# A hybrid encoder layer: all 16 gate jobs of the second batch as 2x2 block products, with their first two products made at the end of the convolutions

## The chip, the cores and the metric

The kernel runs on one core of one Trainium2 chip. The time is device microseconds of one execution. Five engines work in queues of their own: TensorE (PE in the profile, with its weight loads as PEld), VectorE (DVE), ScalarE (ACT), GpSimd (POOL) and SyncE (SP), which here only issues transfers. Each engine takes its instructions in the order in which they stand in its queue.

## What is computed

One encoder layer runs over two batches (prompt and sample, 1024 positions of 1024 channels each). What matters of the reference:

```python
xn = rmsnorm(x, g_pre)
p = xn @ w_in
fv, fg, hv, hg, mg = jnp.split(p, ...)          # Fourier, its gate, Hyena, its gate, merge gates
fz = fft over sequence and channel of fv, real part
y_f = (fz * silu(fg)) @ w_fourier_out
v, x1, x2 = jnp.split(short_conv(hv, w_short), 3, axis=-1)
z = v
for n, gate in enumerate((x1, x2)):
    z = gate * long_conv(z, kf[:, n], hyena_d[n])
y_h = (z * silu(hg)) @ w_hyena_out
g_f, g_h = jnp.split(sigmoid(mg + b_merge), 2, axis=-1)
out = (g_f * y_f + g_h * y_h) @ w_out
y = x + rmsnorm(out, g_post)
```

The change is about the gate columns of `xn @ w_in` for the second batch: the sections 0 (`fg`), 4 (`hg`), 5 and 6 (`mg`), each 1024 channels wide.

## The kernel before

Every float32 product is made of three matmuls on rounded halves (high x high, high x low, low x high). A matrix operand is therefore first split: ACT casts it to the high part (`wh`, `bh`, `yh`), and DVE or POOL subtracts to get the low part (`wl`, `bl`, `yl`). `split` does both.

Three phases follow each other. `phase_fourier` makes the Fourier branch. `phase_main` makes filters and the first batch's gates, and then, in `branches`, the long convolutions of both batches: 16 steps (two orders, eight channel tiles) for each batch. A step is a projection (`inproj`, PSUM tile `pin`), transposes (`tph`), forward transforms (`pX`), a product with the filter on DVE (`t`, `y`), backward transforms (`pT`) and sums on DVE (`S`, `T1s`, `U`, `q`, `ez`, `yc`) up to the gated `x`. `phase_tail` makes the second batch's gates, then four net products (`pn`), then the output rows.

A gate can be made in two ways. `spill_gate` makes one tile (128 channels, 1024 positions) from 48 matmuls with `inproj`, in a `pin` tile: two quarters of four blocks of w_in, each split once for 24 matmuls. A gate job of `phase_tail` makes two tiles (`c`, `c + 1`) as a 2x2 block product with seven products instead of eight, 12 matmuls each: 84. The seven are 11 x B11, 12 x B21, s2 x T2, s1 x T1, s4 x B22, s3 x T3, 22 x T4. The left ones are blocks of w_in and their sums, made by `prepare` from a raw tile `wraw`; B11, B21 and B22 are quarters of the normed input `X` (tiles x0k for the first half of the positions, x1k for the second); T1 to T4 are sums of them, loaded into four `room` tiles. `times` makes one product.

Eight single tiles of the sections 5 and 6, the list `PLAIN`, are made by `spill_gate` in the last four convolution steps and behind them; the other 24 tiles are 12 gate jobs. The block sums of w_out for the last product (`block_sums`, tiles `ws`) are called inside the gate loop.

Most of the program is written in the order of the work, and a scheduler with a model of its own then places the instructions of each engine; it may draw an instruction ahead of others written before it. `issue_after` and `keep_in_program_order` bind it: `times` holds its first matmul in program order, while the `mm3` matmuls of `inproj` are free. Tiles are taken from pools by tag, with a fixed number of buffers (`bufs`); a new tile waits for the last reader of the old one under its tag.

Of the kernel before, what the change touches and what calls it, by code (L numbers as in the profile page):

```python
# [9 lines left out]
F32 = mybir.dt.float32  # L10
# [151 lines left out]
class K:  # L162
# [35 lines left out]
    def setup(self, ctx):  # L198
        tc, nc, a = self.tc, self.nc, self.a
        self.cp = cp = ctx.enter_context(tc.tile_pool(name="cp", bufs=1))  # L200
        self.ps = ctx.enter_context(tc.tile_pool(name="ps", bufs=2, space=bass.MemoryType.PSUM))
        self.dr = ctx.enter_context(tc.tile_pool(name="dr", bufs=1, space=bass.MemoryType.DRAM))

        def ld(name, shape, src, eng=nc.sync):
            t = cp.tile(shape, F32, name=name)
            eng.dma_start(t, src)
            return t
        self.ident = ld("ident", [P, P], a["c_id"], nc.gpsimd)
        self.gpre = ld("gpre", [P, 8], a["g_pre"], nc.gpsimd)
# [20 lines left out]
        self.d_s = [[dt(f"d_s{n}_{p}", [P, 4, 512]) for p in range(7)] for n in range(2)]  # L230
        self.d_wo = [dt(f"d_wo{k}", [P, D]) for k in range(8)]
        self.d_sh = [[dt(f"d_sh{b}_{k}", [P, L]) for k in range(8)] for b in range(NB)]

# [822 lines left out]
            nc.sync.dma_start(self.d_g[b][sec][ct][:, s], t)  # L1056


    def conv_front(self, u, ws):
        nc = self.nc  # L1060
        u4 = u.rearrange("p (n s) -> p n s", n=4)
        eo = ws.tile([P, 2, 4, P], F32, tag="t4", name="eo4", bufs=2)
        self.add("dve", eo[:, 0], u4[:, :, P:2 * P], u4[:, :, P - 1::-1])
        self.sub("dve", eo[:, 1], u4[:, :, P:2 * P], u4[:, :, P - 1::-1])
        xt = ws.tile([P, 2, 4, P], F32, tag="t4", name="xt", bufs=2)
        for e in range(2):
            tp = self.psum("T", 2, "tph")
            for q in range(4):
                nc.tensor.transpose(tp[:, q * P:(q + 1) * P], eo[:, e, q], self.ident)  # L1069
            nc.scalar.copy(xt[:, e].rearrange("p a b -> p (a b)"), tp)  # L1070
        return self.butterfly(ws, xt, xt)
# [133 lines left out]
    def branches(self, nb, nct, ws, mi):  # L1205
# [5 lines left out]
        for b in range(nb):  # L1211
# [4 lines left out]
        plain = list(self.PLAIN)  # L1216
        Z, X, G = {}, {}, {}

        def front(i):
# [34 lines left out]
        for i, (b, n, c) in enumerate(steps):  # L1254
# [20 lines left out]
            if b == 0 and NF <= c:  # L1275
                self.spill_gate(0, 0, c, ws)
        with tc.issue_after(self.ended.ins):
            for sec, c in plain:
                self.spill_gate(1, sec, c, ws)


    def times(self, p, A, B, first):
# [54 lines left out]
    def phase_tail(self):  # L1337
# [10 lines left out]
        with ExitStack() as es:  # L1348
# [7 lines left out]
            def prepare(nm, s, c):  # L1356
# [16 lines left out]
                    A[n] = h, l  # L1373
                if opening:
                    parts("11", wp, ("w", "w"), r[:, 0], 2)
                elif nm == "g" and (s, c) == gates[0]:
                    for j in range(2):
                        t = cell(gw, f"st{j}", "wa", F32R)
                        self.split(t[:, 0], t[:, 1], r[:, j], "dve", "act")
                        A[("11", "12")[j]] = tri(t[:, 0]), tri(t[:, 1])  # L1380
                else:
# [12 lines left out]
                if opening:  # L1394
                    yield A
                parts("s3", gw, ("s3h", "s3l"), r[:, 2], 1)
                if not opening:
                    parts("s1", gw, ("s1h", "s1l"), s, 1)
                yield A
                parts("s4", gw, ("s4h", "s4l"), r[:, 1], 1)  # L1400
                parts("22", gw, ("a2h", "a2l"), r[:, 3], 1)
                yield A

# [6 lines left out]
                self.copied = nc.scalar.copy(t, p)  # L1410
                return t

            def first(A, Y, *where):
                pa, pb = self.psum(*(where or ("mm", 4)), "pg"), self.psum("X", 2, "pg")
# [134 lines left out]
            def at(t, f, *args):  # L1549
                todo.setdefault(t, []).append((f, args))  # L1550
# [59 lines left out]
            prep, ahead = prepare("o", *rows[0]), []  # L1610
            for t in (95, 98, 106, 108):
                at(t, lambda: ahead.append(next(prep)))

            def step(t):
                for v in sorted(x for x in todo if x <= t):
# [78 lines left out]
            A = prepared("g", *gates[0])  # L1694
# [3 lines left out]
            Y = {"B11": [self.X[k][0] for k in range(4)], "B21": [self.X[4 + k][0] for k in range(4)],  # L1698
                 "B22": [self.X[4 + k][1] for k in range(4)]}
# [10 lines left out]
            def part2(out, job, A, Y, pa, pb, m1):  # L1710
# [8 lines left out]
                v = kept(pa)  # L1719
                out(job, 1, 1, pc, v, SUB)  # L1720
                yield pc, u
            pa, pb, m1 = first(A, Y, "T", 2)
            with tc.issue_after(self.copied.ins):
                for j, q in order[2:]:
                    for k in range(2):
                        round_t(rooms[q], k)
            for i, job in enumerate(gates):
                end = i + 1 == len(gates)
                p2 = part2(gate_out, job, A, Y, pa, pb, m1)
                for t in (-3, -2, -1):  # L1730
                    made = next(p2)
                    if end:
                        step(t)
                pc, u = made
                A_, pa_ = A, pa
                if not end:
                    A = prepared("g", *gates[i + 1])
                    pa, pb, m1 = first(A, Y)
# [4 lines left out]
                    if i + 2 == len(gates):  # L1743
                        step(-6)
                else:
                    act, dve = self.rounded.ins.engine, self.left.ins.engine
                    for s in range(2):
                        pinned(product, s)
                        step(s)
                self.times(pa_, A_["s4"], Y["B22"], False)  # L1750
                gate_out(job, 0, 1, pa_, None, None)
                if i + 2 == len(gates):
                    step(-5)
                self.times(pc, A_["22"], Y["T4"], False)
                gate_out(job, 1, 0, pc, u, SUB)
                if i + 2 == len(gates):
                    step(-4)
            for s in range(2, END):
                pinned(product, s)
                step(s)  # L1760
# [3 lines left out]
            with tc.issue_after(self.copied.ins):  # L1764
                load_sum("T4")
                for k in range(2):
                    round_z("T1", k)
                list(prep)
                for k in range(4):
                    round_z("B22", k)  # L1770
                for k in range(2):
# [113 lines left out]
```

## Time and profile before

| | |
|---|---|
| median of 3 runs | 2349.67 us |
| lowest, highest | 2348.7, 2353.85 us |
| span of the profiled execution | 2350.8 us (no other time of it is given, so its span stands for it) |
| instructions | 36414 |
| PE busy | 2326.5 us, 99% |
| DVE busy | 1971.9 us, 84% |
| ACT busy | 1108.7 us, 47% |
| POOL busy | 411.2 us, 17% |

The profile gives each engine's busy time, the share in forty slices of the span, groups of like instructions with their mean duration, and what ended each wait. A table of stretches gives, for each piece of time, the busy time of each engine with its count of instructions, the granted TensorE clock (1.00 is full), the share of the DMA engines and GB/s. A line of the profile can be that of a helper: all matmuls stand on L195, all DVE sums and products on L182. A matmul's row shows 0.39 us for 512 columns, though the next one starts sooner, since matmuls overlap; times of PE are therefore taken from start to start. The same holds, less so, for DVE. The second batch's last convolution steps lie between 1490 and 1626 us, the gate jobs between 1652 and 1882 us.

### The profile page before, as it was taken

To read this page: it belongs to the slowest core of one execution; us is meant where nothing else is said; L and a number is where in the kernel's file an instruction comes from. 1 tells how busy PE (TensorE), PEld (TensorE's weight loads), DVE (VectorE), ACT (ScalarE), POOL (GpSimd) and SP (SyncE) were. 2 spreads that over 40 slices of the span, in tenths; PEclk is the share of its full clock that TensorE was granted. 3 is DMA by queue.
4 is the path that set the end of the run, shared out by engine and by line. 5 is a ranking of instruction groups with operands and counts; after the bars stand their busy time and mean duration, and the time that the engine had idled before them with its cause. 6 is when DMAs were issued, how large, how long until landed. Compare 5 with 4: busy or idle time off the path is not lost.

```text
span 2350.8 us, 36414 instructions
## 1 busy us (share of the span) xinstructions
PE 2326.5 (99%) x12880; PEld 2027.2 (86%) x12880; DVE 1971.9 (84%) x3477; ACT 1108.7 (47%) x2075; POOL 411.2 (17%) x389
## 2 busy tenths in 40 slices
PE   8999999999999999999999999999999999999998
PEld 7999888888888888888888888888888888888787
DVE  7875788888889999999999989988765478777987
ACT  7654667676653333334222223334443465566443
POOL 1002322322443343321000000122000000101311
PEclk9999999999999999999999999999999999999999
DMA  8636865555776667666556555456853688998654
GB/s 275 225 119 226 269 194 169 165 163 183 217 234 203 204 211 216 213 189 233 185 174 178 171 162 169 154 160 223 301 167 126 219 282 269 254 317 246 193 163 143
DMA packets 247360, 479.71 MB, mean 204 GB/s; under 512 B 24710, under 2 KB 82408, under 8 KB 246858
## 3 DMA queue, kind: packets, MB, share of 16 engines
q1 hardware_dynamic: 223165, 402.25, 52.7%
q0 software_dynamic: 23792, 75.11, 11.4%
q8 instruction: 101, 1.65, 0.3%
q14 instruction: 81, 0.66, 0.1%
q10 hardware_dynamic: 221, 0.04, 0.0%
HBM read 326.82 MB, written 177.73 MB: 215 GB/s over the span
## 4 chain that ended last, share of the span: by engine, by line
PE 55%; DVE 2%; DMA 2%; issue 1%; ACT 0%; POOL 0%; DVEq 0%; SPq 0%; POOLq 0%; ACTq 0%
PE pin L195 19%; PE pg L195 16%; PE pn L195 9%; PE pT L195 5%; PE pX L195 5%; PE tph L1069 1%; DMA d_m<-gt 1%; DMA wraw<-d_m 1%; DMA g<-d_g 0%; DVE wl L182 0%; DVE r L182 0%; DVE gt L182 0%; DVE room L182 0%; DMA wl<-d_s 0%; DVE x L178 0%
## 5 line engine op out<-in xcount | busy, mean ns | idle before, releaser
L195 PE MATMUL pin<-x,wh 128*128 128x512 f32 x2816 | 888.9, 391 | 0.0
L195 PEld LDWEIGHTS pin<-x,wh 128*128 128x128 f32 x2816 | 523.3, 188 | 99.1
L195 PE MATMUL pin<-x,wl 128*128 128x512 f32 x1408 | 551.0, 391 | 0.0
L182 POOL TENSOR_TENSOR wl<-wr,wh 128x512 fp32r<-128x512 f32 x128 | 231.0, 1805 | 700.4 <-ACT wh L172 669.5
L195 PEld LDWEIGHTS pin<-x,wl 128*128 128x128 f32 x1408 | 265.0, 188 | 49.8
L195 PE MATMUL pn<-room,wh 128*128 128x512 f32 x864 | 267.5, 391 | 1.0 <-DVE gt L182 0.7
L195 PEld LDWEIGHTS pn<-room,wh 128*128 128x128 f32 x864 | 162.9, 189 | 35.8 <-issue 1.1
L195 PE MATMUL pn<-room,wl 128*128 128x512 f32 x432 | 169.2, 392 | 1.4 <-DVE wl L182 1.4
L195 PE MATMUL pX<-bh,cfwd 128*128 128x256 f32 x768 | 161.6, 289 | 0.4 <-DVE t L182 0.3
L182 DVE TENSOR_TENSOR t<-pX,k 128x1024 f32<-128x1024 f32 x128 | 155.4, 1214 | 7.6 <-DMA k<-d_k 4.0
L195 PE MATMUL pT<-cinv,yh 128*128 128x256 f32 x768 | 145.3, 284 | 0.5 <-DVE T0s L182 0.5
L172 ACT CAST wh<-wr 128x512 fp32r<-128x512 f32 x128 | 79.1, 618 | 123.1 <-PE pin L195 80.0
L172 ACT CAST bh<-b 128x512 fp32r<-128x512 f32 x144 | 88.7, 619 | 96.3 <-DVE b L182 66.7
L195 PEld LDWEIGHTS pX<-bh,cfwd 128*128 128x128 f32 x768 | 126.3, 190 | 3.1 <-DVE t L182 0.7
L195 PEld LDWEIGHTS pT<-cinv,yh 128*128 128x128 f32 x768 | 122.8, 191 | 6.3 <-issue 0.6
L1526 POOL DMA_DIRECT2D d_m<-gt x32 | 27.2, 850 | 535.2 <-DVE gt L182 513.7
L172 ACT CAST yh<-y 128x512 fp32r<-128x512 f32 x96 | 59.5, 620 | 120.4 <-DVE y L182 120.2
L195 PE MATMUL pX<-bl,cfwd 128*128 128x256 f32 x384 | 109.2, 284 | 0.0
L195 PE MATMUL pT<-cinv,yl 128*128 128x256 f32 x384 | 108.9, 284 | 0.0
L182 DVE TENSOR_TENSOR bl<-b,bh 128x512 fp32r<-128x512 f32 x144 | 101.7, 710 | 2.7 <-ACT bh L172 2.5
L195 PEld LDWEIGHTS pn<-room,wl 128*128 128x128 f32 x432 | 81.4, 188 | 19.6 <-DVE wl L182 2.7
L1070 ACT COPY xt<-tph 128x512 f32<-128x512 f32 x64 | 36.9, 587 | 128.6 <-PE tph L1069 128.4
(380 smaller groups left out, 5121.0 us busy)
## 6 DMA issues: line engine op xcount, KB each, us to landing
k<-d_k SPq DMA_DIRECT2D x128, 512.0 KB, 4.2
wr<-in_w_in SPq DMA_DIRECT2D x128, 256.0 KB, 3.7
d_g<-gt SPq DMA_DIRECT2D x124, 256.0 KB, 2.9
wl<-d_s SPq DMA_DIRECT2D x56, 512.0 KB, 5.6
d_k<-kt SPq DMA_DIRECT2D x128, 128.0 KB, 2.4
d_k<-kt SPq DMA_DIRECT2D x64, 256.0 KB, 2.7
g<-d_g SPq DMA_DIRECT2D x64, 256.0 KB, 5.3
r<-d_g SPq DMA_DIRECT2D x60, 256.0 KB, 5.8
```

Source lines behind the costliest of these rows:

```text
L172: self.rounded = nc.scalar.copy(h, src)
L182: return e.tensor_tensor(out, a, b, op=op)
L195: return self.nc.tensor.matmul(out, lhsT, rhs, start=start, stop=stop, skip_group_check=shared)
L1069: nc.tensor.transpose(tp[:, q * P:(q + 1) * P], eo[:, e, q], self.ident)
L1070: nc.scalar.copy(xt[:, e].rearrange("p a b -> p (a b)"), tp)
L1526: nc.gpsimd.dma_start(dst, t, accum_op=ADD)
```

## The change

All 16 gate jobs of the second batch become block products, and PLAIN is gone. `FIRST` lists eight units of two jobs. `spill_first` takes the place of `spill_gate` at the same eight calls (six in the last four convolution steps, two behind them) and makes for two jobs the two products 11 x B11 and 12 x B21 in one `pin` tile: first 12 matmuls for each job (block 11), then ACT copies that partial product and SP stores it to `d_p`, then 12 more for each job on top (block 12), whose sum is the first quarter of the job's output. Each block of 12 has a split of its own, on ACT and POOL. The matmuls go through `times`.

In the tail, `opened` loads the partial product from `d_p` and ACT copies it into PSUM, where the other five products of the job go on. The loop makes s2, s4 of the job before, s3, 22 of the job before, s1, and calls the five parts of `prepare` one by one between them.

```diff
+    def spill_first(self, jobs, ws):
+        nc, a, wp = self.nc, self.a, self.wp
+        ps = self.psum("mm", 2, "pin", L)
+        at = lambda i: ps[:, 512 * i:512 * i + 512]
+        kept = ws.tile([P, L], F32, tag="u", name="m", bufs=1)
+        for q in range(2):
+            for i, (sec, c) in enumerate(jobs):
+                h = wp.tile([P, 4, P], F32R, tag="wh", name="wh", bufs=3)
+                l = wp.tile([P, 4, P], F32R, tag="wl", name="wl", bufs=3)
+                hf, lf = [t.rearrange("p a b -> p (a b)") for t in (h, l)]
+                r = wp.tile([P, 512], F32, tag="w", name="wr", bufs=2)
+                nc.sync.dma_start(r, a["w_in"][sec, c][:, 512 * q:512 * q + 512])
+                self.split(hf, lf, r, "pool", "act")
...
+                self.times(at(i), (h, l), [self.X[4 * q + k][0] for k in range(4)], q == 0)
+                if q == 0:
+                    m = kept[:, 512 * i:512 * i + 512]
+                    nc.scalar.copy(m, at(i))
+                    nc.sync.dma_start(self.d_p[sec, c], m)
...
             for _ in range({4: 1, 3: 1, 2: 2, 1: 2}.get(len(steps) - i, 0)):
-                self.spill_gate(b, *plain.pop(), ws)
+                self.spill_first(units.pop(0), ws)
...
-    PLAIN = [(5, 0), (5, 1), (6, 0), (6, 1), (5, 2), (5, 3), (6, 2), (6, 3)]
+    FIRST = [((s, c), (s, c + 2)) for s in (5, 6, 0, 4) for c in (0, 4)]
...
-        gates = [(s, c) for c in range(0, 8, 2) for s in (0, 4, 5, 6) if (s, c) not in self.PLAIN]
+        gates = [(s, c) for c in range(0, 8, 2) for s in (0, 4, 5, 6)]
...
+            def opened(job):
+                m = wp.tile([P, 512], F32, tag="wh", name="m1", bufs=3)
+                nc.sync.dma_start(m, self.d_p[job])
+                p = self.psum("mm", 4, "pg")
+                nc.scalar.copy(p, m)
+                return p
...
+                ahead_of()
+                self.times(pa, A["s2"], Y["T2"], False)
...
+                if past:
+                    job_, A_, pa_, pc_, u_ = past
+                    self.times(pa_, A_["s4"], Y["B22"], False)
+                    gate_out(job_, 0, 1, pa_, None, None)
...
+                self.times(pc, A["s3"], Y["T3"], True)
...
+                if past:
+                    self.times(pc_, A_["22"], Y["T4"], False)
+                    gate_out(job_, 1, 0, pc_, u_, SUB)
...
+                self.times(pa, A["s1"], Y["T1"], False)
```

The order of the instructions changes from the last six convolution steps on. On PE the two orders part in the middle of a backward transform; `pin` is a projection, `x` the normed input. Before:

```order
L195 MATMUL pin<-x_0_13053,wh 128x512 x2
L195 MATMUL pin<-x_0_13053,wl 128x512
L195 MATMUL pin<-x_1_13061,wh 128x512 x2
L195 MATMUL pin<-x_1_13061,wl 128x512
L195 MATMUL pin<-x_2_13069,wh 128x512 x2
L195 MATMUL pin<-x_2_13069,wl 128x512
L195 MATMUL pin<-x_3_13077,wh 128x512 x2
L195 MATMUL pin<-x_3_13077,wl 128x512
L195 MATMUL pin<-x_0_13057,wh 128x512 x2
L195 MATMUL pin<-x_0_13057,wl 128x512
L195 MATMUL pT<-cinv,yh 128x2x128 x2
L1069 MATMUL tph<-ident,eo_16776 128x128 x4
```

The same place on PE now, from the last row that both have:

```order
L195 MATMUL pin<-x_7_13129,wl 128x512
L195 MATMUL pT<-cinv,yh 128x2x128 x2
L1102 MATMUL tph<-ident,eo_16792 128x128 x4
L195 MATMUL pX<-bh,cfwd 128x256
L195 MATMUL pX<-bl,cfwd 128x256
```

No `pin` stands in the 196 matmuls after that one, up to and with the third backward transform (`pT`) from there; 264 of them stand between there and the last backward transform, and 216 behind it, where 140 stood.

On DVE the block sums of w_out (`ws`) come in between the operations of the last step but one. The place before, behind the butterfly sums `b`:

```order
L182 TENSOR_TENSOR b_17758<-xt,bs 128x256
L182 TENSOR_TENSOR b_17758<-bs,xt 128x2x128 x2
L182 TENSOR_TENSOR yl<-y,yh 128x512
L182 TENSOR_TENSOR bl<-b_17758,bh 128x512
L182 TENSOR_TENSOR T0s<-pT_17856,T0s 128x256
```

And now:

```order
L182 TENSOR_TENSOR b_17808<-xt,bs 128x256
L182 TENSOR_TENSOR b_17808<-bs,xt 128x2x128 x2
L182 TENSOR_TENSOR ws_19108<-ws_19108 128x512
L182 TENSOR_TENSOR ws_19108<-ws_19108,ws_19109 128x512
L178 SCALAR_TENSOR_TENSOR ws_19109<-ws_19108,ws_19109 128x512
L182 TENSOR_TENSOR ws_19228<-ws_19228 128x512
L182 TENSOR_TENSOR ws_19109<-ws_19109 128x512
L182 TENSOR_TENSOR ws_19228<-ws_19228,ws_19229 128x512
L178 SCALAR_TENSOR_TENSOR ws_19229<-ws_19228,ws_19229 128x512
L182 TENSOR_TENSOR yl<-y,yh 128x512
```

Seven of the 16 sums stand there in a row, and the other nine follow singly up to the end of the convolutions.

On SP the place is the end of the single tiles or units, where the first gate job's weights (`wraw`) and the rooms are loaded; `wr` is the weights of a single tile, `d_sh` the convolution's output, `d_g` a finished gate. Before:

```order
L1363 DMA wraw_18572<-in_w_in 128x1024 x2
L1429 DMA fz_18662<-d_fz1_0_100 128x512
L1429 DMA fz_18710<-d_fz1_1_101 128x512
L1363 DMA wraw_18715<-in_w_in 128x1024 x2
L1274 DMA d_sh1_7_285<-x2_17841 128x1024
L1017 DMA wr_18511<-in_w_in 128x512
L1056 DMA d_g1_6_0_180<-gt_18403 128x512
L1056 DMA d_g1_6_0_180<-gt_18406 128x512
L1583 DMA room0_18568<-d_t0_1_241 128x1024 x2
```

Now, where `r30` and `r31` are inputs of the first net product, `m` and `m1` partial products on their way to and from `d_p`, and `wl_20513` a weight of the first net product, loaded into the tile of x05:

```order
L1080 DMA d_p4_6_277<-m_18632 128x512
L1492 DMA r30_20587<-d_g0_0_5_129 128x512
L1492 DMA r31_20588<-d_g0_0_6_130 128x512
L1492 DMA r31_20588<-d_g0_0_7_131 128x512
L1447 DMA m1_18874<-d_p4_0_274 128x512
L1526 DMA wl_20513<-d_s0_0_248 128x1024
L1396 DMA wraw_18748<-in_w_in 128x1024 x2
L1085 DMA fz_18716<-d_sh1_6_300 128x512
L1622 DMA room0_18744<-d_t0_1_241 128x1024 x2
```

The first job's weights and the rooms moved from ahead of the last single tiles to behind all units' loads and behind `wl_20513`, which waits for the sixth matmul of the last 12 of the last unit.

More of the change, by code (lines that the diff above doesn't have):

```diff
@@ L1056, in spill_gate @@
             nc.sync.dma_start(self.d_g[b][sec][ct][:, s], t)
+    def spill_first(self, jobs, ws):
[11 more added lines that the diff above has]
+                self.split(hf, lf, r, "pool", "act")
+                self.pooled = self.left
+                self.times(at(i), (h, l), [self.X[4 * q + k][0] for k in range(4)], q == 0)
[3 more added lines that the diff above has]
+                    nc.sync.dma_start(self.d_p[sec, c], m)
+        for i, (sec, c) in enumerate(jobs):
+            t = wp.tile([P, 512], F32, tag="gt", name="gt", bufs=3)
+            if sec in (0, 4):
+                f = wp.tile([P, 512], F32, tag="gt", name="fz", bufs=3)
+                nc.sync.dma_start(f, (self.d_sh if sec else self.d_fz)[1][c][:, 0:512])
+                nc.scalar.activation(t, at(i), AF.Silu)
+                self.mul("dve", t, t, f)
+            else:
+                nc.scalar.copy(t, at(i))
+            nc.sync.dma_start(self.d_g[1][sec][c][:, 0:512], t)
     def conv_front(self, u, ws):
@@ L1277, in branches @@
         with tc.issue_after(self.ended.ins):
-            for sec, c in plain:
-                self.spill_gate(1, sec, c, ws)
+            for jobs in units:
+                self.spill_first(jobs, ws)
     def times(self, p, A, B, first):
@@ L1375, in prepare @@
                     parts("11", wp, ("w", "w"), r[:, 0], 2)
[L1376 to L1381, printed above, removed]
+                elif nm == "o":
                     parts("11", wp, ("wh", "wl"), r[:, 0], 3)
@@ L1393, in prepare @@
                 parts("s2", gw, ("s2h", "s2l"), r[:, 0], 1)
-                if opening:
+                if opening or nm == "g":
                     yield A
                 parts("s3", gw, ("s3h", "s3l"), r[:, 2], 1)
+                if nm == "g":
+                    yield A
                 if not opening:
@@ L1411, in kept, with first @@
                 return t
-            def first(A, Y, *where):
-                pa, pb = self.psum(*(where or ("mm", 4)), "pg"), self.psum("X", 2, "pg")
+            def opened(job):
[4 more added lines that the diff above has]
+                return p
+            def first(A, Y):
+                pa, pb = self.psum("mm", 4, "pg"), self.psum("X", 2, "pg")
                 self.times(pa, A["11"], Y["B11"], True)
@@ L1609, in phase_tail @@
                 at(109 + k, round_z, "T3", k)
-            prep, ahead = prepare("o", *rows[0]), []
+            opening, ahead = prepare("o", *rows[0]), []
             for t in (95, 98, 106, 108):
-                at(t, lambda: ahead.append(next(prep)))
+                at(t, lambda: ahead.append(next(opening)))
             def step(t):
@@ L1693, in phase_tail @@
             rooms = [gs.tile([P, 2, 4, 512], F32R, tag=f"t{q}", name=f"room{q}", bufs=1) for q in range(4)]
-            A = prepared("g", *gates[0])
+            prep = prepare("g", *gates[0])
+            next(prep), next(prep)
             act, dve = self.rounded.ins.engine, self.left.ins.engine
@@ L1697, in phase_tail @@
                 load_t(rooms[q], 0, int(j[1]) - 1)
-            Y = {"B11": [self.X[k][0] for k in range(4)], "B21": [self.X[4 + k][0] for k in range(4)],
-                 "B22": [self.X[4 + k][1] for k in range(4)]}
+            Y = {"B22": [self.X[4 + k][1] for k in range(4)]}
             for j, q in order[:2]:
@@ L1721, in part2 @@
                 yield pc, u
[L1722 to L1726, printed above, removed]
-            for i, job in enumerate(gates):
[L1728 to L1732, printed above, removed]
-                        step(t)
[L1734 to L1738, printed above, removed]
+            A, pa = list(next(prep) for _ in range(2))[-1], opened(gates[0])
@@ new lines, in phase_tail, with mark @@
+            for j, q in order[2:]:
+                for k in range(2):
+                    round_t(rooms[q], k)
+            past = None
+            for i, job in enumerate(gates):
+                to = i + 1 - len(gates)
+                more = prepare("g", *gates[i + 1]) if to else None
+                ahead_of = (lambda: next(more)) if to else (lambda: None)
+                def mark(n):
+                    t = n - 5 + 5 * to
+                    if t >= -6:
+                        step(t)
+                ahead_of()
+                self.times(pa, A["s2"], Y["T2"], False)
+                u = wp.tile([P, 512], F32, tag="wl", name="u", bufs=3)
+                nc.scalar.copy(u, pa)
+                ahead_of()
+                mark(0)
+                if past:
+                    job_, A_, pa_, pc_, u_ = past
+                    self.times(pa_, A_["s4"], Y["B22"], False)
+                    gate_out(job_, 0, 1, pa_, None, None)
+                next(prep)
+                mark(1)
+                pc = self.psum("T", 2, "pg")
+                self.times(pc, A["s3"], Y["T3"], True)
+                ahead_of()
+                mark(2)
+                if past:
+                    self.times(pc_, A_["22"], Y["T4"], False)
+                    gate_out(job_, 1, 0, pc_, u_, SUB)
+                next(prep)
+                mark(3)
+                self.times(pa, A["s1"], Y["T1"], False)
+                v = kept(pa)
+                gate_out(job, 1, 1, pc, v, SUB)
+                B = ahead_of()
+                past = job, A, pa, pc, u
+                if to:
+                    A, pa, prep = B, opened(gates[i + 1]), more
@@ L1742, in phase_tail @@
                                         [a["w_out"][(i - 2 + 4 * j) * P:(i - 1 + 4 * j) * P] for j in range(2)])
[L1743 to L1757, printed above, removed]
+                mark(4)
+            for s in range(2):
+                pinned(product, s)
+                step(s)
+            job_, A_, pa_, pc_, u_ = past
+            self.times(pa_, A_["s4"], Y["B22"], False)
+            gate_out(job_, 0, 1, pa_, None, None)
+            self.times(pc_, A_["22"], Y["T4"], False)
+            gate_out(job_, 1, 0, pc_, u_, SUB)
             for s in range(2, END):
@@ L1767, in phase_tail @@
                     round_z("T1", k)
-                list(prep)
+                list(opening)
                 for k in range(4):
```

5 lines of the change are left out of this document (4 added, 1 removed).

## Prediction

> **What bounds it now.** I read the page first, then a table of stretches around the place that the change touches, then the waits of VectorE, then single rows.
>
> ```profile
> PE 2326.5 (99%) x12880; PEld 2027.2 (86%) x12880; DVE 1971.9 (84%) x3477; ACT 1108.7 (47%) x2075; POOL 411.2 (17%) x389
> ...
> PE   8999999999999999999999999999999999999998
> ...
> DVE  7875788888889999999999989988765478777987
> ...
> L182 POOL TENSOR_TENSOR wl<-wr,wh 128x512 fp32r<-128x512 f32 x128 | 231.0, 1805 | 700.4 <-ACT wh L172 669.5
> ...
> L172 ACT CAST wh<-wr 128x512 fp32r<-128x512 f32 x128 | 79.1, 618 | 123.1 <-PE pin L195 80.0
> ...
> wr<-in_w_in SPq DMA_DIRECT2D x128, 256.0 KB, 3.7
> ```
>
> TensorE (PE) is busy 99% of the span and shows no gap from slice 2 to slice 39, so a matmul that goes is worth its full time, and so is every microsecond for which PE has nothing to do. But VectorE (DVE) stands at nine tenths and more all through the convolutions: there it is a second engine almost as full. The table of stretches puts numbers on that place (second batch's last convolutions, their end, and the gate jobs):
>
> ```profile
> core 0: us, PE busy (x) PEld busy (x) DVE busy (x) ACT busy (x) POOL busy (x), PEclk, DMA share, GB/s
> 1490.03:1537.00 46.97, 46.97 (x291) 42.20 (x290) 46.38 (x78) 14.36 (x28) 6.17 (x6) 1.00 0.58 178
> 1537.00:1620.00 83.00, 83.00 (x506) 74.15 (x506) 69.75 (x116) 27.46 (x52) 19.26 (x13) 1.00 0.44 141
> ...
> 1657.00:1880.00 223.00, 223.00 (x985) 184.73 (x984) 134.11 (x207) 90.62 (x157) 0.00 (x0) 1.00 0.59 194
> ```
>
> In the first row DVE works 46.38 of 46.97 us: it is the bound there as much as PE. PE is full only because single gate tiles are mixed in. The last row is the old gate stage: 984 matmuls by the code (12 jobs of 84, less the opening 24) in 223.0 us, 0.2266 us each, with DVE at 60% and ScalarE (ACT) at 41%.
>
> **What goes.** Before: 8 single tiles of 48 matmuls and 12 jobs of 84, 1392. After: 16 jobs of 24 early and 60 late, 1344. That is 48 fewer, 48 x 0.2266 = **-10.9 us**.
>
> In the late loop a job is 13.6 us of PE. Its DVE work falls (two splits and one sum fewer, about 134.1/12 - 3 x 0.6 = 9.4 us), and ACT has one filling of PSUM more and three rounds and copies fewer, so both stay under 13.6 and I charge nothing there.
>
> **The convolutions lose their filler.** The next rows cut out the `pin` matmuls (convolution inputs and single gate tiles together), and give the start of the place where the two orders part, on PE and on DVE.
>
> ```profile
> 1487.77:1537.00 49.23, 30.99 (x129) 23.24 (x127) 5.08 (x4) 3.31 (x4) 1.00 0.58 178
> 1537.00:1620.00 83.00, 52.01 (x213) 38.85 (x214) 2.54 (x2) 5.38 (x9) 1.00 0.44 141
> ```
> ```profile
> 1487.77 0.62 PE L195 MATMUL pin<-x,wh 128*128 128x512 f32 x2
> ...
> 1500.47 1.05 PE L195 MATMUL pT<-cin,y 128*128 128x128 f32 x8
> 1501.28 0.48 PE L195 MATMUL pT<-cinv,yh 128*128 128x256 f32 x2
> ...
> 1616.56 0.40 PE L195 MATMUL pT<-cinv,yh 128*128 128x256 f32 x2
> ...
> 1616.92 0.40 PE L195 MATMUL pT<-cinv,yh 128*128 128x256 f32 x2
> ...
> 1619.64 0.40 PE L195 MATMUL pT<-cinv,yh 128*128 128x256 f32 x2
> ```
> ```profile
> 1490.03 1.27 DVE L178 SCALAR_TENSOR_TENSOR x<-pin,wsh,x 128x1023 f32<-128x1023 f32 x1
> ...
> 1516.68 1.23 DVE L182 TENSOR_TENSOR t<-pX,k 128x1024 f32<-128x1024 f32 x1
> 1517.82 0.68 DVE L182 TENSOR_TENSOR bl<-b,bh 128x512 fp32r<-128x512 f32 x1
> 1518.42 0.68 DVE L182 TENSOR_TENSOR S<-T1s,pT 128x512 f32<-128x512 f32 x1
> ...
> 1519.62 0.41 DVE L182 TENSOR_TENSOR b<-xt 128x256 f32<-128x256 f32 x1
> 1519.96 0.68 DVE L182 TENSOR_TENSOR T1s<-T1s,pT 128x512 f32<-128x512 f32 x1
> ```
>
> Before, 129 pins (29.2 us) stand between 1487.77 and 1537. In the new order there is not one: `times` holds the first matmul of each early product in program order, so the filler can no longer be drawn ahead of the convolution it is written behind. From 1487.77 to the third inverse transform (`pT`) PE has 156 matmuls 256 wide and 40 transposes and others 128 wide: 0.12 each (1616.56 to 1616.92 is three) and 0.10 each (0.81 for eight), 22.7 us, ready to end at 1510.5. DVE, from 1490.03 to the split `yl` which that transform reads, still has 37 operations of 512 at 0.60, 12 of 1023 or 1024 at 1.14 to 1.19, 30 of 256 at 0.34 and 4 of 128: 47 us, so 1537. PE must wait 1537 - 1510.5 - about 1 for the mixing, **25 us**, and no engine can shorten it. Then, to the last transform, PE has 264 pins (59.8 us) and the other transforms (in the second row 83.0 - 213 x 0.2266 = 34.8 us, less the 3.7 that it now did sooner: 31), so it ends at 1628 when nothing else waits, where 78 pins fewer without a wait would give 1620 - 17.7 = 1602: the same 25 us. DVE has its 69.75 us of the second row and 16 new operations, the block sums of w_out that moved in from the gate stage (16 x 0.60 = 9.6): 79 in 91, room enough, but not where it is needed:
>
> ```profile
> DVE S L182 <- PE pT L195: 7.7, 2, 5.5
> DVE b L182 <- ACT xt L1070: 4.6, 1, 4.6
> ```
>
> Long blocks of pins now stand ahead of transforms (72 in a row, then 33 and 39 around a transpose), and DVE waits behind such blocks already now, 12.3 us in these two rows. Then it is late for the last step, and SP loads the sums' rows only when the last convolution input has left its tiles. I give 0 to 8 for it and take 3: the stage costs **28 us** (25 to 33), and the last transform ends near 1631 instead of 1620.
>
> **216 pins in one run.** Behind that stand 18 blocks of 12 pins (48.9 us, already in the count). Each block needs a split of its own, where a split served 24 before: two `wr` buffers, each turned round in 3.7 (load) + 0.62 (ACT) + 1.8 (POOL) = 6.1 us, so one in 3.06 us against 2.72 of PE. Over 18 blocks 6 us, less the three that can be ready: 0 to 6, I take **3**. Each POOL split beside DVE also holds a DVE operation; 16 more of them lie mostly where DVE is free, nothing. The new copies and stores of `m` (16 each) are behind PE and hide under the next block.
>
> **The gate jobs open late.** Before, the first job's weights and T2's room are loaded under 96 single-tile matmuls:
>
> ```profile
> 1623.05 0.80 SPq L1363 DMA_DIRECT2D wraw<-in_w_in  x2
> ...
> 1632.02 5.22 SPq L1583 DMA_DIRECT2D room<-d_t  x8
> ```
> ```profile
> 1634.61 0.68 DVE L182 TENSOR_TENSOR s2l<-wraw,s2h 128x512 fp32r<-128x512 f32 x1
> ...
> 1640.75 1.22 DVE L182 TENSOR_TENSOR room<-room 128x1024 fp32r<-128x1024 f32 x1 [0.63 <-ACT room L172]
> ```
> ```profile
> 1657.20 0.62 PE L195 MATMUL pg<-room,s2h 128*128 128x512 f32 x2
> ```
> ```profile
> room<-d_t SPq DMA_DIRECT2D x8, 512.0 KB, 9.7
> wraw<-in_w_in SPq DMA_DIRECT2D x6, 512.0 KB, 5.7
> ```
> ```profile
> 1627.00:1657.00 30.00, 30.00 (x134) 24.82 (x134) 18.73 (x24) 16.19 (x25) 3.48 (x3) 1.00 1.02 383
> ```
>
> From the load at 1623.05 to `s2l` it takes 12.2 us, from the rooms' issue to T2 rounded 9.9, and 34 us lie between the load and PE's first use. After, SP reaches `wraw` only behind `wl<-d_s`, a load of the next stage into tile x05, which the last block of pins still reads up to its sixth matmul: 6 x 0.2266 = 1.4 us before the pins end. Weights, rooms and all behind them on SP's queue then start at that point, and PE has no matmul left: its next is s2 x T2. By the weights' path it starts 12.2 - 1 = 11 us after the last pin, by the room's (issued 2.5 us later) also 11, and DVE has both and one gate product in one line: I take 12, with 8 and 14 as ends. Then the second job: up to its weights SP has some 7.3 MB in line, 18 to 19 us at 383 GB/s, and DVE needs 7 operations (4.2 us) from there to `s2l`, so 22 to 24 us after the last pin; PE, with 36 matmuls (8.2 us) to do from 12 on, is there at 20.2. I take 3 (0 to 5). Together **15 us** (8 to 19).
>
> **Clock.** PE gaps have a second price, which the trace shows once, at the end of the nets:
>
> ```profile
> 2176.53 0.70 PE L195 MATMUL pn<-room,wh 128*128 128x512 f32 x2 [0.72 <-DVE gt L182]
> 2178.30 0.50 PE L195 MATMUL pn<-room,wl 128*128 128x512 f32 x1 [1.07 <-DVE wl L182]
> ```
> ```profile
> 2178.00:2180.00 2.00, 1.70 (x5) 1.33 (x6) 1.97 (x4) 0.28 (x1) 0.25 (x1) 0.76 1.04 420
> 2180.00:2182.00 2.00, 2.00 (x6) 1.60 (x5) 1.97 (x4) 0.06 (x1) 0.85 (x1) 0.50 1.05 374
> 2182.00:2184.00 2.00, 2.00 (x9) 1.60 (x9) 2.00 (x3) 2.00 (x3) 0.84 (x1) 0.89 1.07 286
> ```
>
> After two gaps of together 1.8 us the granted clock is 0.76, 0.50 and 0.89 in three pieces of 2 us: 2 x (0.24 + 0.50 + 0.11) = 1.7 us lost. The new order has the two gaps at the opening and a broken stretch in the convolutions; I charge three such spells, **5 us**, with 1.7 and 7 as ends.
>
> The Trainium skill (TensorE: Matmul & The Clock Gate, HAM oscillation — how this bites in real kernels) sets the limit at PE gaps of more than about 3.4 us; by it the short gaps in the convolutions and the second one at the opening would cost nothing, one spell would be left, and the sum would be 3 us lower. Here two gaps of 0.7 and 1.1 us were enough, so I follow the trace.
>
> **Sum.** 2350.8 - 10.9 + 28 + 3 + 15 + 5 = 2390.9 us. The profiled span lies 1.1 us above the median of the runs, 2349.67, so the time to expect is **2390 us**, 1.7% slower. With all low ends 2350.8 - 10.9 + 25 + 0 + 8 + 1.7 - 1.1 = 2373.5, with all high ends 2350.8 - 10.9 + 33 + 6 + 19 + 7 - 1.1 = 2403.8.
>
> **Rivals.**
>
> Faster, with all 48 matmuls paid out: 2349.7 - 10.9 = 2339. PE was 99% busy, and work that only moves leaves its sum as it was. For this DVE's 47 us before the third transform would have to become 22, or PE's queue would have to hold other work there; the row of 46.38 in 46.97 us and the order speak against it. It decides when all of PE's new gaps together stay under 10.9 us.
>
> The convolutions stall, the opening doesn't: the loads behind x05 then arrive before PE's pins end, if PE is held up so long by the splits that SP is through its line. 2349.7 - 10.9 + 28 + 3 + 1.7 = 2371. Against it stands that the wait is for a matmul 1.4 us before the end, whenever that is.
>
> The opening stalls, the convolutions don't, because DVE's backlog at 1490 is smaller than the order reads: 2349.7 - 10.9 + 3 + 15 + 3.4 = 2360.
>
> Worse than forecast: the halved clock stays on through the broken stretch and the transforms, at 0.24 us for 0.12, become the chain themselves. PE's 22.7 us there double to 45 and no longer hide behind DVE's 47; 10 to 20 us more, 2400 to 2410.
>
> **Chances.** The forecast, both stalls, 0.70 (its own range 2373 to 2404); convolutions alone 0.10; opening alone 0.05; worse 0.06; faster 0.06; 0.03 for gains and gaps that cancel. A measurement of this kernel tells some 0.2% from no change: slower 0.70 + 0.10 + 0.05 + 0.06 = 0.91, within it 0.03, faster 0.06. The range, 2362 to 2412, runs from the convolutions' case at its low end to the worse case, and leaves out most of the opening-alone and the faster case.
>
> **What would show it.** Right: PE busy falls from 99% to about 97%; in slices 25 to 28 it shows eights or less, with PE's waits there put down to DVE `yl`, `b` and `bl`; one PE gap of some 12 us before the first `pg<-room,s2h`, with the load of `wraw` issued within 2 us of the last `pin`; a granted clock under 1 there; 48 matmuls fewer; 13.6 us a job afterwards. The splits' term is wrong if the `pin` run after the last transform takes 49 us flat. The forecast is wrong if PE stays full from 1490 to the end of the pins, or if `wraw` lands before them. The nets and the output rows should stand as before, 2 us either way.

## The result, and the profile after

The changed kernel takes 2408.09 us (median; 2407.22 to 2409.04) against 2350.6 for the one before: ratio 1.0245 [1.0231, 1.026], 2.4% slower. The forecast was 2390, range 2362 to 2412. The profiled execution has a span of 2406.8 us, 56.0 more than before.

The page after, its sums for PE and its slices:

```profile
PE 2334.6 (97%) x12832; PEld 2029.2 (84%) x12832; DVE 1985.6 (83%) x3485; ACT 1129.0 (47%) x2111; POOL 420.6 (17%) x405
...
PE   8999999999999999999999999898699999999998
...
DVE  7875788798889999999999999983566578788887
...
PEclk9999999999999999999999999899899999999999
```

PE fell below nine tenths in slices 26, 28 and 29 (a slice is 60 us): the part of the convolutions that was left without filler (the bare stretch below), the run of pins with the last transforms, and the opening of the gate jobs; slice 29 is the 6. PE's waits from 1450 us on, grouped (us in total, times, longest), and two stretches:

```profile
PE pg L195 <- ACT s2h L172: 14.7, 2, 13.1
PE pin L195 <- ACT m L1079: 10.4, 8, 2.4
PE pT L195 <- DVE yl L182: 6.4, 4, 3.1
PE pT L195 <- ACT yh L172: 5.5, 4, 2.0
PE pX L195 <- DVE t L182: 5.3, 3, 4.6
```
```profile
1490.00:1537.00 47.00, 32.51 (x193) 29.94 (x192) 46.24 (x84) 14.04 (x28) 3.55 (x5) 0.75 0.37 123
...
1700.00:1730.00 30.00, 13.68 (x45) 9.68 (x44) 21.03 (x27) 17.04 (x24) 0.00 (x0) 0.72 1.04 408
```

The second line of waits was in no term of the forecast: matmuls of an early product that wait for ScalarE's copy `m`. Landmarks on PE: the last matmul that both orders have in common, the first `pin` after the bare stretch, the last transform, the last `pin`, the first gate matmul, the first net matmul:

```profile
1489.52 0.39 PE L195 MATMUL pin<-x,wl 128*128 128x512 f32 x1
...
1541.32 0.63 PE L195 MATMUL pin<-x,wh 128*128 128x512 f32 x2
...
1638.97 0.28 PE L195 MATMUL pT<-cinv,yl 128*128 128x256 f32 x1
...
1700.65 0.39 PE L195 MATMUL pin<-x,wl 128*128 128x512 f32 x1
...
1714.17 1.22 PE L195 MATMUL pg<-room,s2h 128*128 128x512 f32 x2 [13.13 <-ACT s2h L172]
...
1933.25 0.62 PE L195 MATMUL pn<-n,wh 128*128 128x512 f32 x2
```

Before, these stood at 1487.54 (the last common matmul), 1619.88 (last transform), 1651.54, 1651.77 and 1874.81. This execution was thus 2.0 us late before the orders parted; the other versions below stand between -2.5 and 2.5 us there, so this is scatter and not the change. The time between two landmarks, less its matmuls at 0.2266 us, is what a stage lost. For the convolutions it is the delay of the last transform less this early lateness, and with it the `pin` matmuls that moved behind the transform (76 here, 17.2 us). So the 56.0 us are: 2.0 from ahead of the change, 34.3 in the convolutions (19.1 - 2.0 + 17.2), 12.7 in the 216 pins (61.7 - 48.9), 13.3 in the gap, 7.0 in the gate loop (219.1 for 936 matmuls, 212.1), less 10.9 for the 48 matmuls and less 2.4 in the nets and rows.

This table has the same working for all versions. "At the start" is how late that same matmul was against the kernel before; "behind" is all that was lost from the last transform to the first net matmul. These three columns are of the profiled executions, which in free_tail4 and pool_queue took 5 and 6 us more than the median.

| kernel | at the start | convolutions | behind | median, us | ratio to before |
|---|---|---|---|---|---|
| changed | 2.0 | 34.3 | 33.0 | 2408.09 | 1.0245 [1.0231, 1.026] |
| bind_plain | -0.2 | 32.3 | 1.2 | 2383.09 | 1.0139 [1.0124, 1.0154] |
| free_fill | -1.4 | 8.8 | 27.1 | 2375.17 | 1.0098 [1.008, 1.0116] |
| sums_late | -1.0 | 27.9 | 37.4 | 2405.98 | 1.0232 [1.0219, 1.0246] |
| two_tiles | 0.6 | 34.8 | 24.8 | 2400.88 | 1.0212 [1.0198, 1.0227] |
| pair_units | 0.1 | 33.9 | 39.3 | 2413.8 | 1.0271 [1.0256, 1.0287] |
| hold_loads | 0.9 | 35.9 | 34.0 | 2410.76 | 1.0252 [1.0236, 1.0267] |
| tail_units | 0.7 | 35.6 | 23.6 | 2399.89 | 1.0209 [1.0195, 1.0223] |
| free_tail | -2.5 | 1.6 | 24.8 | 2364.1 | 1.0056 [1.0042, 1.007] |
| free_tail4 | 2.5 | 5.5 | 27.1 | 2369.55 | 1.0082 [1.0068, 1.0096] |
| pool_queue | -1.0 | 2.0 | 30.0 | 2366.26 | 1.0074 [1.006, 1.0088] |
| four_plain | -0.2 | 1.9 | 14.4 | 2362.35 | 1.0052 [1.0039, 1.0064] |
| four_plain_two | -1.4 | 2.2 | 4.5 | 2351.68 | 1.0001 [0.9992, 1.001] |

### The profile page after: what moved, and what is told of

Same layout as the page of the kernel before. It is cut to its first block, busy times and chain, and to the rows that moved or that the text cites. A ratio compares the mean times of both kernels' runs of the same rounds, so it can differ in the third digit from the quotient of the medians.

```text
span 2406.8 us, 36474 instructions
## 1 busy us (share of the span) xinstructions
PE 2334.6 (97%) x12832; PEld 2029.2 (84%) x12832; DVE 1985.6 (83%) x3485; ACT 1129.0 (47%) x2111; POOL 420.6 (17%) x405
## 5 line engine op out<-in xcount | busy, mean ns | idle before, releaser
L195 PE MATMUL pin<-x,wh 128*128 128x512 f32 x2816 | 888.5, 392 | 10.4 <-ACT m L1079 10.4
L182 POOL TENSOR_TENSOR wl<-wr,wh 128x512 fp32r<-128x512 f32 x144 | 246.2, 1710 | 713.4 <-ACT wh L172 683.4
L172 ACT CAST wh<-wr 128x512 fp32r<-128x512 f32 x144 | 89.0, 618 | 159.9 <-PE pin L195 111.3
L1565 POOL DMA_DIRECT2D d_m<-gt x32 | 27.1, 848 | 536.4 <-DVE gt L182 508.6
L1302 POOL CAST mark<-x 128x1 fp32r<-128x1 f32 x30 | 24.4, 814 | 433.0 <-DVE x L178 432.8
L178 DVE SCALAR_TENSOR_TENSOR x<-pin,wsh,x 128x1023 f32<-128x1023 f32 x64 | 81.6, 1275 | 19.9 <-ACT x L1037 11.1
```

Of the source, the lines that this page charges most:

```text
L172: self.rounded = nc.scalar.copy(h, src)
L178: return self.nc.vector.scalar_tensor_tensor(out, a, s, b, op0=op0, op1=op1)
L182: return e.tensor_tensor(out, a, b, op=op)
L195: return self.nc.tensor.matmul(out, lhsT, rhs, start=start, stop=stop, skip_group_check=shared)
L1302: with tc.issue_after(nc.gpsimd.tensor_copy(mark, z[:, 0:1]).ins):
L1565: nc.gpsimd.dma_start(dst, t, accum_op=ADD)
```

## Experiments

**The lost filler.** bind_plain is the kernel before with one thing of the change: in `spill_gate`, for the eight single tiles, the first matmul of each block of 12 is bound.

```diff
+                        if bound and kk == 0:
+                            m = self.mm(ps[:, s], h[:, kk], self.X[k][n][0], k == 0, False)
+                            self.tc.keep_in_program_order(m)
...
```

> The kernel before, its eight single tiles still made as 48 matmuls each, but the first matmul of every block of 12 held in program order, as the changed kernel holds it. Theory (the lost filler is the larger part of the loss, and the binding alone loses it): the matmuls of the single tiles leave the stretch from 1490 us to the third inverse transform, PE waits there for VectorE about 22 to 27 us in all, and the time is 2380 us (2373 to 2388). Rival (the block sums of w_out that VectorE got in the convolutions, or the shorter splits, made the stall): no sums move here, so the time stays at 2351 (2349 to 2356).

2383.09 us. Its stretch and its largest waits:

```profile
1490.00:1537.00 47.00, 30.36 (x191) 27.57 (x189) 46.92 (x86) 12.69 (x26) 2.05 (x4) 0.82 0.40 129
```
```profile
PE pT L195 <- ACT yh L172: 11.3, 7, 2.2
PE pT L195 <- DVE yl L182: 6.5, 4, 3.1
```

Neither a new split nor a block product is in it, and 32.3 us are lost in the convolutions, with 1.2 behind. The binding alone is enough for a loss of that size. free_fill is the opposite: the changed kernel with `times(..., bound=False)` for the early products.

> The changed kernel, the matmuls of the early products no longer held in program order. Theory: the filler comes back, the 22 us of PE waits between 1490 and 1541 and the 6.5 us behind it go; the first gate's weights also stand ahead of the load of the next stage on SP's queue, which gives back some 5 us of the opening. 2367 us (2357 to 2375). Rival (VectorE's work there is a wall whatever PE has to do): the waits only move behind the convolutions and the time stays above 2395.

2375.17 us, just above the expected range. PE is full again where it had waited, and what the opening costs stayed. The first gate's weights did go out ahead of the load of the next stage (1665.45 against 1684.18), but only as the last `pin` ended, and no 5 us came back:

```profile
1490.00:1537.00 47.00, 46.63 (x295) 41.92 (x294) 45.45 (x78) 17.18 (x35) 9.54 (x9) 1.00 0.60 192
...
1677.19 1.22 PE L195 MATMUL pg<-room,s2h 128*128 128x512 f32 x2 [11.69 <-ACT s2h L172]
```

**The block sums.** sums_late holds them in the gate loop (`pinned(self.block_sums, ...)`).

> The changed kernel, the sixteen block sums of w_out held back into the gate loop, where they were before. Theory (they delay VectorE in the last steps: the wait of 4.6 us for t at 1605 and those of 0.7, 0.2 and 1.0 us behind it are theirs): PE's waits between 1590 and 1640 fall from 6.5 to under 2 us, 2403 us (2400 to 2405). Rival (VectorE is late there from the blocks of matmuls that stand ahead of the transforms, not from the sums): the waits stay, 2406 to 2410.

The wait of 4.6 us and its like went (2.7 us of waits are left there), and the convolutions lost 6.4 us less (34.3 to 27.9). But in the gate loop the sums' 9.6 us of VectorE and their transfers cost 4.9 us (11.9 lost there in place of 7.0), and the median fell by 2.1 only, with intervals of the two ratios that overlap. The theory was right about the place, the rival near in time: the sums make VectorE late there, and moved away they are paid for elsewhere.

**The copies.** Why PE waits for `m` in the changed kernel, in rows of all engines:

```profile
1662.28 0.60 ACT L1086 ACTIVATE gt<-pin 128x512 f32<-128x512 f32 x1 [1.45 <-DVE gt L182]
...
1662.78 0.61 ACT L172 CAST wh<-wr 128x512 fp32r<-128x512 f32 x1
...
1663.29 0.59 ACT L1079 COPY m<-pin 128x512 f32<-128x512 f32 x1
...
1663.92 0.73 PE L195 MATMUL pin<-x,wh 128*128 128x512 f32 x2 [1.35 <-ACT m L1079]
```

The next block goes into the other half of the same PSUM tile, and the program makes it wait until ScalarE has copied the first half; the copy stands behind a `gt` and a cast on ScalarE's queue. There are eight such waits in this run, 10.4 us (the two texts below, written before their runs, speak of nine and of 11.6). pair_units let blocks of two units take turns:

> The changed kernel, the last four units made two at a time: the blocks of two units take turns, so that between a block and the next block into the same PSUM tile stands a block of another tile. Nothing else moves. Theory (PE's next block waits for ScalarE's copy of the partial product, because both lie in one PSUM tile, although in different halves): seven or eight of the nine waits of 0.7 to 2.4 us go, 2397 us (2394 to 2400). Rival (the copy's wait stands in front of the wait for the split on POOL, whose cycle of about 3.06 us for a block bounds the run anyway): the waits turn into waits for the split, 2405 to 2409.

2413.8 us, against both theories. The waits for `m` fell to 1.4 us and the 216 pins took 5.5 us less, but the finished outputs of four jobs now came together; ScalarE stood behind them (its row before the copy waits 8.7 us for a product on VectorE, which waits for a load), and with it the copy of the first job's partial product into PSUM:

```profile
PE pg L195 <- ACT pg L1484: 29.7, 1, 29.7
```

So it told little of the copies. two_tiles left the order alone and gave each job of the last four units a PSUM tile of its own:

```diff
...
+        tiles = [self.psum("mm", 2, "pin", L) for _ in range(2 if two else 1)]
+        at = lambda i: tiles[i if two else 0][:, 512 * i:512 * i + 512]
...
```

> The changed kernel, with one edit for the last four units: the two jobs of a unit lie in two PSUM tiles in place of the two halves of one. PE's order of matmuls is the same, and so are the copies, their buffers and their stores. Theory (the nine waits for the copies, 11.6 us, come from the shared tile and nothing else): at most two short ones stay, the last pin ends 9 us sooner, and since the opening begins with the end of the matmuls it keeps its length: 2399 us (2396 to 2402). Rival (the splits' cycle is the bound of this run and the copies only stand in front of it): the waits become waits for POOL's or ScalarE's parts of the split, 2405 to 2410.

2400.88 us, as the theory had it, with three short waits in place of two. All of PE's waits from 1640 to 1720:

```profile
PE pg L195 <- ACT s2h L172: 15.9, 2, 13.9
PE pg L195 <- DVE s2l L182: 1.7, 1, 1.7
PE pin L195 <- ACT m L1079: 1.5, 3, 0.6
PE pin L195 <- ACT gt L1086: 0.2, 1, 0.2
```

The run of pins lost 2.9 us in place of 12.7. No `pin` in it waits for a part of a split (`wh` or `wl`), so the rival is out: the splits' cycle does not bound this run. The opening, gap and loop, cost 21.9 us in place of 20.3.

**The opening.** The forecast blamed a load ahead of the first weights on SP (`wl` at 1700.51, `wraw` at 1701.29). hold_loads issues the next stage's loads behind the rooms.

> The changed kernel, the loads of the next stage (inputs and weights of the first net product) issued behind the last load of the rooms. PE's order is the same. Theory (SP stands at the load that waits for the last block of matmuls, and the first gate's weights behind it): the weights go out at about 1696.5 us in place of 1701.3, PE's gap of 13.1 us before the first s2 falls to about 8.5, 2403 us (2400 to 2406). Rival (the weights' landing, the rooms' and VectorE's chain are set by the transfers in flight and not by the place in the queue): the gap stays, 2407 to 2409.

2410.76 us, above both ranges and by the intervals no different from the changed kernel. The weights went out at 1696.13, and the gap shrank as the theory had it, but the second and third jobs waited instead:

```profile
1696.13 0.92 SPq L1396 DMA_DIRECT2D wraw<-in_w_in  x2
```
```profile
1709.07 1.22 PE L195 MATMUL pg<-room,s2h 128*128 128x512 f32 x2 [7.55 <-ACT s2h L172]
...
1723.14 0.73 PE L195 MATMUL pg<-room,s2h 128*128 128x512 f32 x2 [1.92 <-ACT s2h L172]
```
```profile
1700.00:1730.00 30.00, 18.51 (x61) 13.54 (x60) 21.56 (x28) 17.71 (x26) 0.00 (x0) 0.77 1.03 393
```

Gap and loop together lost 21.3 us (7.7 + 13.6) against 20.3 (13.3 + 7.0). In both kernels the DMA engines are full from 1700 to 1730, at 408 and 393 GB/s: some 12 MB in these 30 us. The place on the queue set the gap, as the theory said, but not the price: it only said who waits. tail_units starts these loads under the last four units, which it writes in the gate stage behind them, one PSUM tile for each job:

> The changed kernel, its last four units written in the gate stage behind the loads of the first jobs' weights and the rooms, each of their jobs in a PSUM tile of its own; matmuls held in program order as before. The convolutions up to the last transform keep their order. Theory (the opening's cost is that some 12 MB begin to load only when PE's matmuls end, whatever stands in front on SP, and the copies' waits come from two jobs in one tile): loads and rounding lie under the 192 matmuls, the gap of 13.1 us and the later ones of the opening go (20 us), and the copies' waits behind the convolutions too (10 us): 2378 us (2373 to 2386). Rival (transfers of the opening collide with those of the units and of the next stage, at 400 GB/s, and the gap only moves): 2395 or more.

2399.89 us, the rival: the gap before the first s2 was gone, but now the cover waited: the units' weights stood behind the opening's loads.

```profile
PE pg L195 <- ACT wh L172: 12.9, 1, 12.9
```

**All three mended.** free_tail frees the early matmuls, puts the last two units into the gate stage and the sums into its loop; free_tail4 puts four units there.

> Three edits together: the early products' matmuls free in the convolutions, the last two units in the gate stage behind the first loads with one PSUM tile for each job, the block sums of w_out back in the gate loop. Theory (the three stalls are the whole loss, and the 48 matmuls are worth their time once PE is full): the gain of 10.9 us stays, less some 3 for the remaining copies' waits, 2343 us (2338 to 2350), faster than before. Rival (with 48 matmuls fewer something else, VectorE in the convolutions or the transfers of the opening, takes the gain): 2350 to 2362.

> As the one with three edits, but the last four units stand in the gate stage, and their matmuls are free too. Theory: fewer copies' waits, since only four units keep two jobs in one tile, and the last convolutions hold 48 matmuls of filler in place of 72: 2342 us (2337 to 2350). Rival (too little filler in the last step: PE waits there for VectorE): 2348 to 2358.

2364.1 and 2369.55 us, worse than either rival. In free_tail the convolutions lose next to nothing (1.6 us), and 24.8 us are lost behind; on SP the opening's loads (4 `wraw`, 8 of rooms) come ahead of a unit's weights, and PE waits for these:

```profile
1629.36 2.30 SPq L1394 DMA_DIRECT2D wraw<-in_w_in  x4
1631.71 2.31 SPq L1637 DMA_DIRECT2D room<-d_t  x4
...
1642.49 1.66 SPq L1480 DMA_DIRECT2D wr<-in_w_in  x2
```
```profile
1651.93 1.22 PE L195 MATMUL pg<-x,wh 128*128 128x512 f32 x2 [6.91 <-ACT wh L172]
```

pool_queue loads the units' weights on POOL's queue.

> The version with three edits (free_tail), with the loads of the units' weights issued on POOL's queue in place of SP's. Theory (the units' weights were late because they stood behind 6 MB of the opening's loads on one queue): the wait of 6.9 us for ScalarE's wh at 1652 and that of 1.6 for POOL's wl go, 2355 us (2351 to 2359). Rival (all transfers share 400 GB/s, and the weights are late from the traffic itself, or POOL, which must issue loads between its splits, gets late): 2362 to 2372.

2366.26 us, the rival's time, though neither of its two reasons is what the longest wait shows. The wait for `wh` at this place fell to 0.8 us, and PE waited 6.0 us for a low part instead: POOL took 6.66 us over that split, where its neighbours take 1.29, while VectorE worked without a pause:

```profile
1649.54 6.66 POOL L182 TENSOR_TENSOR wl<-wr,wh 128x512 fp32r<-128x512 f32 x1 [13.02 <-ACT wh L172]
...
1656.25 0.79 PE L195 MATMUL pg<-x,wl 128*128 128x512 f32 x1 [6.02 <-POOL wl L182]
```

No version with this queue moved that split off POOL, so what the queue alone is worth stays open.

four_plain changes the cover itself: seven units, then four single tiles as before the change, whose split serves 24 matmuls.

> The changed kernel with the early products' matmuls free, and the last unit replaced by four single tiles (section 6, channels 4 to 7, 48 matmuls each, one split for 24) behind the convolutions: seven units, 14 gate jobs, 1368 matmuls, 24 fewer than before. Theory (a split, a load and a store for every 12 matmuls, where one load served 24 before, fill SP's queue and the transfers just when the opening's 12 MB must load; single tiles as cover leave room for them): the opening shows no gap over 2 us, the convolutions one or two copies' waits, 2348 us (2343 to 2352), at or just under before. Rival (the opening stalls whatever covers it, since the partial products' loads and copies come on top): a gap of 5 us and more stays before the first s2, 2354 to 2362.

2362.35 us, the rival's time with the theory's opening. The gap before the first s2 is 2.0 us and the gates lose 5.1 in all, but 9.3 are lost in the 280 pins: waits for copies (4.2 us, of them one in the convolutions), and this, on POOL and PE:

```profile
1650.53 1.29 POOL L182 TENSOR_TENSOR wl<-wr,wh 128x512 fp32r<-128x512 f32 x1 [1.43 <-ACT wh L172]
1660.34 9.95 POOL L182 TENSOR_TENSOR wl<-wr,wh 128x512 fp32r<-128x512 f32 x2 [8.52 <-ACT wh L172]
```
```profile
1668.64 0.50 PE L195 MATMUL pin<-x,wl 128*128 128x512 f32 x1 [2.35 <-POOL wl L182]
```

four_plain_two mends both: two tiles for a unit, and VectorE for the four tiles' low parts.

> The version with four single tiles at the end (four_plain), with two more edits: the units behind the convolutions with one PSUM tile for each job, and the low parts of the four single tiles made on VectorE in place of POOL, whose two took 9.95 us together at 1660 beside VectorE's work. Theory: the copies' waits (4.2 us) and the wait for POOL (2.4 us) go, some 2 us of lost clock with them, 2354 us (2351 to 2358). Rival (VectorE, which rounds the rooms and the first job's weights there, then opens the gate jobs later): 2358 to 2364. By neither is it faster than before.

2351.68 us, ratio 1.0001: no difference from before, and at the good end of the theory's range. Its transfers are as dense as ever, and PE is full under them, since the first weights went out at 1641.31, 47 us ahead of the first s2:

```profile
1641.31 0.90 SPq L1399 DMA_DIRECT2D wraw<-in_w_in  x2
```
```profile
1690.00:1720.00 30.00, 30.00 (x134) 24.85 (x133) 21.68 (x34) 13.04 (x23) 0.00 (x0) 1.00 1.04 389
```

Its 24 matmuls fewer are worth 5.4 us; 6.7 are lost by the table, and the rest is the scatter at the start and in the nets. No version beat the kernel before.

## Why the prediction was right, and where it was short

The direction held, and so did the main case, both stalls; the forecast was 18 us short. The time lies above the main case's own range, 2373 to 2404; it lies inside the full one because that reached up to the worse rival, whose halved clock is not what made it longer, so that part was luck. Against its sum the profile is 15.9 us longer: 6.3 in the convolutions, 9.7 in the pins, 5.3 in the opening, 2.0 from ahead of the change, less 2.4 in the nets and rows and less the 5 for the clock, whose price is inside the other stages. By its own steps:

- **48 matmuls, -10.9.** No run shows it alone. The balance above closes to 56.0 with it.
- **The convolutions, 28 (25 for the filler, 3 for lateness).** 34.3 measured. The filler's part was right in mechanism and near in size: without the sums' delay 27.9 are lost, and PE got its first `pin` at 1541.3, which, less the 2.0 us of late start, is 2.3 us after the 1537 worked out from VectorE's operations. The lateness was mis-sized: with the sums moved away 6.4 us less are lost, where 3 were taken out of a range of 0 to 8. The forecast saw that the sums' 9.6 us had room but not where it was needed; that seven of them stood ahead of a `yl` was shown and not priced.
- **216 pins, 3.** 12.7 measured, and both terms failed. The 3 us were for the splits, one in 3.06 us against 2.72 of PE; but no `pin` waits for a split here, nor in two_tiles, where the copies are out of the way. That two_tiles still loses 2.9 us there is a likeness by luck: its four waits are for copies and for a `gt`. The other step is "The new copies and stores of `m` (16 each) are behind PE and hide under the next block". The copies stand in front of it, since both halves are one tile: they were put at nothing and are the only waits among these pins, of whose 12.7 us the two tiles took away 9.8.
- **The opening, 15.** 20.3 measured, 13.3 in the gap (12 forecast) and 7.0 in the loop. The load into x05 does set the gap: without it ahead of the weights, in hold_loads, the gap is 7.7. It does not set the price, for there the later jobs waited instead and gap and loop cost 21.3. What the opening needs is some 30 us of full transfers, and they began as the cover ended. That this is bytes alone, and not also VectorE's chain of rounding, no run separates.
- **Clock, 5.** Near in size, other in place. In the convolutions' bare stretch the granted clock was 0.75 in the mean, some 23 of 47 us at half, and by the row that cost nothing of its own: VectorE was full throughout (46.24 us), and PE's 25 us there became 14.5 of waits and 10 of slow matmuls. At the opening the first 12 matmuls took 5.7 us besides a wait, in place of 2.7: 2.9 lost, which are part of the loop's 7.0. Behind the wait of 4.6 us the clock was at 0.51 from 1605.8 to 1609.3, at most 1.7 us, part of the 34.3.

```profile
1700.00:1704.00 4.00, 1.04 (x5) 0.54 (x3) 0.69 (x1) 1.68 (x3) 0.00 (x0) 1.00 1.06 406
1704.00:1706.00 2.00, 0.00 (x0) 0.00 (x0) 0.00 (x0) 0.59 (x1) 0.00 (x0) 0.70 1.04 424
...
1714.00:1721.00 7.00, 5.16 (x11) 3.65 (x12) 7.00 (x10) 5.83 (x7) 0.00 (x0) 0.50 1.03 408
```
```profile
1660.00:1700.00 40.00, 33.25 (x141) 25.58 (x140) 6.24 (x6) 11.87 (x22) 12.85 (x10) 1.00 0.63 202
```

The clock fell 3.9 us after the last pin ended (1.2 of the 2 us at half speed give 0.70), and gaps of 0.7 to 1.4 us every few microseconds left it at 1.00. The Trainium skill (TensorE: Matmul & The Clock Gate, HAM oscillation — how this bites in real kernels) puts the limit at some 3.4 us without work; here both agree with it. The row of two short gaps in the kernel before, on which the forecast leaned, does not, and neither does the bare stretch: its longest wait is 3.1 us, and the clock was at half for some 23 of its 47 us.

## What to carry to other kernels

Before you read a stage's loss out of two profiles, compare them ahead of the change: here that moved single stages by up to 2.5 us. Before you bind matmuls to program order, ask which of them were filling someone else's wait: a table by stretches that shows two engines full side by side is the warning, since the one then stalls for all that the other has left. When a step needs more loads and copies for the same matmuls, look at what the step had been hiding, and price the copies as part of PE's chain unless they read another PSUM tile. Mending one stall often showed the next behind it; here three had to go together, and what was left of the gain was nothing.

## What was not expected of the hardware

In four_plain a POOL split, of a kind that takes 1.29 us in the rows beside it, released PE 8.3 us after its start (1660.34 to 1668.64), and in pool_queue one took 6.66 us. VectorE made roundings of 1024 columns there, one close behind the other, and the split ended 1.1 us after the last of them, when VectorE had nothing to do (rows of four_plain):

```profile
1659.38 2.35 DVE L182 TENSOR_TENSOR room<-room 128x1024 fp32r<-128x1024 f32 x2
...
1662.85 4.62 DVE L182 TENSOR_TENSOR room<-room 128x1024 fp32r<-128x1024 f32 x4
1668.44 0.70 DVE L182 TENSOR_TENSOR wsum<-wraw 128x512 f32<-128x512 f32 x1 [0.97 <-DMA wraw<-in_w_in]
```

Moving the four single tiles' splits to VectorE was part of what took 10.7 us off. The Trainium skill (SBUF — State Buffer, SBUF: two separate sides) tells of one pair of ports that VectorE and GpSimd lock against each other for a whole instruction. The rows agree that one stands still while the other works, but here the split stood still through a whole run of VectorE's instructions and not through one. A second surprise was that a clock halved for 23 us looks free where another engine is the bound; no run separates it.
